# Output projection of the sliding-window layer as seven half-size products, with their operands summed during the attention

## The chip, the cores and the metric

The kernel runs on one core of a Trainium2 chip. A core has a matrix engine (TensorE, PE in the profile; PEld is its weight load), VectorE (DVE), ScalarE (ACT), GpSimd (POOL) and SyncE (SP), which here only issues DMA transfers. Each engine works through its own list of instructions in order and waits on semaphores for the others. Matmuls read from SBUF and accumulate in the eight banks of PSUM. The metric is the time of one execution in microseconds; lower is better.

## What is computed

Two layers over x of 1024 x 1024, fp32. Only the second is changed much:

```python
# even layer: RG-LRU heads and stick-breaking attention heads, gated, concatenated
y = concat([a_h * silu(a_g), o_b * silu(b_g)]);  x = LN(alpha * x + y @ w_out)      # w_out 2048 x 1024
# odd layer: 16 heads of 64, window 128, 2 key/value heads, sinks, ALiBi
q, k, v, g = split(x @ w_in)
p = softmax_with_sink(q @ k.T / 8 - slope * dist)                                      # inside the window
y = (p @ v) * silu(g);                               x = LN(alpha * x + y @ w_out)      # w_out 1024 x 1024
```

The kernel keeps fp32 precision by splitting each matmul operand into a high part h (rounded) and a low part l = raw - h, and adding three matmuls: h h, h l and l h (`mm3`, lines 110 to 112).

## The kernel before, in words

Data are in tiles of 128 partitions. A "slot" is one of 24 tiles of 128 x 2 x 512 that most operands share. The stages in order of time:

1. Projections of the even layer, its recurrent heads, and then eight heads of stick-breaking attention (`attn_all`). Each unit of a head is one score tile: three matmuls (L326 to 328), two sigmoids on ACT (L333), a running product on DVE (L342) and a product (L344); two units later the tile is transposed on PE (L352) and split (L118, L119). Between units a generator (`fill.pump`) feeds matmuls of other work to PE: the next head's projections, and in head 7 the first product of the output projection (`early_out`).
2. The even output projection (16 x 128 rows of w_out) is done as seven products of half size after Strassen and Winograd: `PRODUCTS` lists for each the y operand, the weight operand and one of two groups of four PSUM banks (X, Z). Sums of y pieces (`y_sums`) and of w_out pieces (`w_sums`, L268 to 283: four loads, five POOL operations, an ACT cast) are made during the attention, w_sums(n) late in head n, and stored to DRAM (`stash`). `prep(k)` loads the two operands of step k, casts the high parts on ACT (L541) and subtracts the low parts on DVE (y) and POOL (weights) (L543), nine steps ahead of `step_mm`. Normalisation of a row block: `bn_stats`, `bn_aggr`, square root, ACT scaling (L662), POOL multiplication by gamma (L663), DVE addition of beta (L668).
3. The odd layer: projections, then `swa_all`: eight pairs of heads with eight query blocks (units) each. A unit is four score matmuls (L900, L901), bias and maximum on DVE (L906), exponentials on ACT (L913), normalising on POOL (L918); three units later transposes on PE (L928) and the split pth / ptl (L118 on ACT, L119 on DVE), one unit later the attention matmuls (L946, L949). After two units the output is copied (L954), added (L957) and multiplied by its gate into the tile yo (POOL, L959). The fillers are the gate projection og of the same pair and the query projection oq of the next.
4. The odd output projection: the eight yo tiles are split (L1017 on ACT, L1018 on DVE), then 8 row blocks x 8 pieces of w_out x 2 column halves x 3 = 384 matmuls. Its first column half is mixed into pair 7 by the scheduler; the second goes row block by row block, each followed by its normalisation (L623 to L654), the last row block in two pieces of 256 columns.

The order of instructions on each engine is set when the kernel is built, by a scheduler that simulates the program; the loops only give the priorities.

Of the kernel before, what the change touches and what calls it, by code (L numbers as in the profile page):

```python
# [52 lines left out]
def trunk(ctx, tc, x, xT_in, w_even, w_even_v, w_even_out, w_gate, lru_vec,  # L53
# [560 lines left out]
    def out_proj(w_src, es, yh, n_tail, tail_piece, lnp, gb, after, name, final):  # L614
        def parts(s):
            return 4 if final and s == NS - 1 else 2

        stats = {s: lnp.tile([P, parts(s), 6], F32, tag=f"st{s}", name=f"st{name}{s}", bufs=1) for s in range(NS)}

        def evac(dm, s, ps, cols=(0, HALF)):  # L620
            c0, c1 = cols
            xt = xpre[:, s, dm * HALF + c0:dm * HALF + c1]
            nc.vector.scalar_tensor_tensor(out=xt, in0=xt, scalar=ALPHA, in1=ps[:, c0:c1], op0=ALU.mult, op1=ALU.add)  # L623
            w = D // parts(s)
            for c in range(0, c1 - c0, w):
                nc.vector.bn_stats(stats[s][:, (dm * HALF + c0 + c) // w, :], xt[:, c:c + w])

        def ln_a(s):
# [4 lines left out]
            return mv, rs  # L633

        def ln_b(s, mv, rs):
            nc.vector.reciprocal(rs[:, 0:1], rs[:, 0:1])
# [1 line left out]
            nmr = None
            if final and s == NS - 1:
                nmr = nc.vector.scalar_tensor_tensor(out=rs[:, 1:2], in0=mv[:, 0:1], scalar=-1.0, in1=rs[:, 0:1],  # L640
                                               op0=ALU.mult, op1=ALU.mult)
                a = slice(LNC, D)
                nc.scalar.activation(xt[:, a], xt[:, a], AF.Identity, bias=rs[:, 1:2], scale=rs[:, 0:1])
                nc.gpsimd.tensor_tensor(out=xt[:, a], in0=xt[:, a], in1=gb[:, 0, a], op=ALU.mult)
                nc.gpsimd.tensor_tensor(out=xt[:, a], in0=xt[:, a], in1=gb[:, 1, a], op=ALU.add)
            if final:
                edges = (0, LNC // 2, LNC) if s == NS - 1 else (0, 512, 1024)
                for c0, c1 in zip(edges, edges[1:]):
                    cs = slice(c0, c1)
                    m = nc.vector.scalar_tensor_tensor(out=xt[:, cs], in0=xt[:, cs], scalar=mv[:, 0:1],  # L650
                                                       in1=gb[:, 0, cs], op0=ALU.subtract, op1=ALU.mult)
                    if c0:
                        order(m, nmr)
                    nc.vector.scalar_tensor_tensor(out=xt[:, cs], in0=xt[:, cs], scalar=rs[:, 0:1], in1=gb[:, 1, cs],  # L654
                                                   op0=ALU.mult, op1=ALU.add)
                    after(s, cs)
                if s == NS - 1:
                    after(s, slice(LNC, D))
                return
            nc.vector.scalar_tensor_tensor(out=rs[:, 1:2], in0=mv[:, 0:1], scalar=-1.0, in1=rs[:, 0:1],  # L660
                                           op0=ALU.mult, op1=ALU.mult)
            nc.scalar.activation(xt, xt, AF.Identity, bias=rs[:, 1:2], scale=rs[:, 0:1])  # L662
            nc.gpsimd.tensor_tensor(out=xt, in0=xt, in1=gb[:, 0, :], op=ALU.mult)  # L663
# [418 lines left out]
```

## Time and profile before

| | us |
|---|---|
| median of 3 runs (lowest to highest) | 1248.36 (1248.14 to 1249.49) |
| profiled execution | 1249.23 |
| its span | 1247.5 |
| PE busy | 1223.2 (98%) |
| DVE, ACT, POOL busy | 849.5 (68%), 627.2 (50%), 623.5 (50%) |
| chain that ended last | PE 88%, DVE 6%, ACT 3% |

The mean granted clock of the execution is 0.998, so PE runs at 2.4 GHz nearly everywhere. The 16 DMA engines are half idle or more except where large operands move. Busy shares are means over stages; the stretches of 10 or 20 us below show where PE is idle.

### The profile page before, as it was taken

Reading aid. Unit: us, or ns where it says so; the run is one execution under the profiler, and the core shown is the slowest. Engines: PE = TensorE matmul, PEld = TensorE weight load, DVE = VectorE, ACT = ScalarE, POOL = GpSimd, SP = SyncE. Lnnn points to the kernel's source line nnn. Section 1 sums busy time; section 2 is a strip of 40 time slices with the busy share of each in tenths; the row PEclk is TensorE's granted clock in tenths of the full one; section 3 lists DMA queues with packets and bytes.
Section 4 is the critical chain, followed back from the end, with each engine's and each line's share of the span. In section 5 each row is a group of like instructions: output and inputs, shape, how many; then the busy total and the mean of one; then the engine's idle time right before and its main releaser. Section 6 shows DMA issues by size and latency. Waiting matters only on the chain.

```text
span 1247.5 us, 18450 instructions
## 1 busy us (share of the span) xinstructions
PE 1223.2 (98%) x6176; PEld 1035.3 (83%) x6176; DVE 849.5 (68%) x1705; ACT 627.2 (50%) x1291; POOL 623.5 (50%) x720
## 2 busy tenths in 40 slices
PE   8999999999999999999999899999999999999997
PEld 6888788888888888888888788888888888887886
DVE  8465666557776776767767728586468778778377
ACT  5255565556443443434444436444367777778300
POOL 3344354435536465554551647567346555555440
PEclk9999999999999999999999999999999999999999
DMA  7312433235515245254353988701111111111022
GB/s 258 123 56 80 148 106 106 91 108 183 172 51 186 92 168 180 74 181 154 109 178 132 383 328 300 249 26 43 43 44 35 34 35 34 28 34 61 21 81 102
DMA packets 88943, 150.16 MB, mean 120 GB/s; under 512 B 10128, under 2 KB 27920, under 8 KB 88592
## 3 DMA queue, kind: packets, MB, share of 16 engines
q1 hardware_dynamic: 88848, 148.98, 35.6%
q8 instruction: 49, 0.80, 0.3%
q14 instruction: 46, 0.38, 0.1%
HBM read 104.90 MB, written 44.04 MB: 119 GB/s over the span
## 4 chain that ended last, share of the span: by engine, by line
PE 88%; DVE 6%; ACT 3%; issue 1%; DMA 1%; POOL 0%; POOLq 0%; SPq 0%; ACTq 0%; DVEq 0%
PE pjv L110 2%; PE tr L352 2%; PE pjv L111 2%; PE pjv L112 2%; PE opeX L554 2%; PE pj_k L110 2%; PE pj_q L110 2%; PE pj_q L112 2%; PE opeX L555 2%; PE pj_k L112 2%; PE pj_k L111 2%; PE pj_q L111 2%; PE pj_g L111 2%; PE opeX L556 2%; PE pj_g L112 2%; PE pj_g L110 2%
## 5 line engine op out<-in xcount | busy, mean ns | idle before, releaser
L333 ACT ACTIVATE C<-z 128x512 f32<-128x512 f32 (+3 forms) x96 | 47.4, 494 | 107.6 <-DVE z L330 67.5
L918 POOL TENSOR_SCALAR S<-S,sm 128x256 f32<-128x256 f32 (+1 forms) x128 | 59.7, 481 | 70.1 <-DVE sm L916 23.9
L543 POOL TENSOR_TENSOR opwl<-rawwl,opwl 128x512 fp32r<-128x512 f32 x48 | 69.4, 1459 | 42.3 <-ACT opwl L541 25.3
L913 ACT ACTIVATE S<-S,sm 128x256 f32<-128x256 f32 (+1 forms) x128 | 62.5, 489 | 48.9 <-DVE sm L909 46.9
L344 DVE TENSOR_TENSOR B<-B,C 128x512 f32<-128x512 f32 (+3 forms) x96 | 75.0, 783 | 9.9 <-DVE wt L119 0.2
L342 DVE TENSOR_TENSOR_SCAN C<-C,one 128x512 f32<-128x512 f32 (+1 forms) x64 | 62.2, 973 | 21.2 <-ACT C L333 21.1
L342 DVE TENSOR_TENSOR_SCAN C<-C,C,one 128x512 f32<-128x512 f32 x32 | 44.1, 1378 | 30.0 <-ACT C L333 30.0
L543 DVE TENSOR_TENSOR opwh<-rawwh,opwh 128x512 fp32r<-128x512 f32 x48 | 51.5, 1101 | 16.0 <-ACT opwh L541 13.6
L118 ACT CAST wt<-tr 128x512 fp32r<-128x512 f32 (+3 forms) x96 | 46.4, 484 | 30.5 <-PE tr L352 30.0
L119 DVE TENSOR_TENSOR wt<-tr,wt 128x512 fp32r<-128x512 f32 (+3 forms) x96 | 52.3, 547 | 7.4 <-ACT wt L118 7.0
L110 PE MATMUL pjv<-wv,xh 128*128 128x512 f32 x128 | 49.6, 399 | 6.4 <-ACT wv L219 4.8
L381 POOL TENSOR_TENSOR yb<-pvt,yb 128x128 f32<-128x128 f32 x32 | 16.1, 503 | 76.2 <-DVE pvt L380 76.2
L541 ACT CAST opwh<-rawwh 128x512 fp32r<-128x512 f32 x48 | 29.8, 621 | 47.2 <-DMA rawwh<-stS 27.8
L110 PE MATMUL pj_g<-xh,wh_g 128*128 128x512 f32 x128 | 52.6, 411 | 0.0
L110 PE MATMUL pj_k<-xh,wh_k 128*128 128x512 f32 x128 | 51.9, 405 | 0.0
L110 PE MATMUL pj_q<-xh,wh_q 128*128 128x512 f32 x128 | 51.8, 405 | 0.0
L112 PE MATMUL pj_g<-xh,wl_g 128*128 128x512 f32 x128 | 51.8, 405 | 0.0
L110 PE MATMUL pj_oq<-x1h,wh_oq 128*128 128x512 f32 x128 | 51.6, 404 | 0.0
L110 PE MATMUL pj_og<-x1h,wh_og 128*128 128x512 f32 x128 | 51.5, 402 | 0.0
L111 PE MATMUL pj_og<-x1l,wh_og 128*128 128x512 f32 x128 | 50.8, 397 | 0.0
L112 PE MATMUL pj_og<-x1h,wl_og 128*128 128x512 f32 x128 | 50.7, 396 | 0.0
L111 PE MATMUL pjv<-wv,xh 128*128 128x512 f32 x128 | 50.7, 396 | 0.0
(333 smaller groups left out, 4386.6 us busy)
## 6 DMA issues: line engine op xcount, KB each, us to landing
vst<-vhl SPq DMA_DIRECT2D x16, 512.0 KB, 4.1
rawwh<-stS SPq DMA_DIRECT2D x32, 256.0 KB, 3.7
rawwl<-stT SPq DMA_DIRECT2D x32, 256.0 KB, 4.5
xraw<-in_xT_dram SPq DMA_DIRECT2D x16, 256.0 KB, 5.4
wvraw<-in_w_even_v_dram SPq DMA_DIRECT2D x16, 256.0 KB, 4.6
wr_ax<-in_w_even_dram SPq DMA_DIRECT2D x16, 256.0 KB, 2.7
wr_ag<-in_w_even_dram SPq DMA_DIRECT2D x16, 256.0 KB, 2.7
stA11p<-a SPq DMA_DIRECT2D x8, 512.0 KB, 2.8
```

The costliest lines, as they stand in the source:

```text
L110: nc.tensor.matmul(ps, wh, xh, start=start, stop=False)
L111: nc.tensor.matmul(ps, wh, xl, start=False, stop=False)
L112: nc.tensor.matmul(ps, wl, xh, start=False, stop=stop)
L118: nc.scalar.copy(h, ps)
L119: nc.vector.tensor_tensor(out=l, in0=ps, in1=h.bitcast(F32), op=ALU.subtract)
L333: nc.scalar.activation(C[:, :W], z[:, :W], AF.Sigmoid, scale=-SC)
L342: nc.vector.tensor_tensor_scan(cr, cr, one.broadcast_to([P, W]), init, ALU.mult, ALU.mult)
L344: nc.vector.tensor_tensor(out=B[:, :W], in0=B[:, :W], in1=C[:, 1:W + 1], op=ALU.mult)
L541: nc.scalar.copy(hl[:, 0, :], raw)
L543: eng.tensor_tensor(out=hl[:, 1, :], in0=raw, in1=hl[:, 0, :].bitcast(F32), op=ALU.subtract)
L913: nc.scalar.activation(Sb[:, j, lo:], Sb[:, j, lo:], AF.Exp, bias=nm[:, j:j + 1], accum_out=den[:, j:j + 1])
L918: nc.gpsimd.tensor_scalar(out=Sb[:, j, lo:], in0=Sb[:, j, lo:], scalar1=rec[:, j:j + 1], scalar2=0.0, op0=ALU.mult, op1=ALU.add)
```

## The change

The odd output projection (1024 x 1024 by 1024 x 1024) becomes seven products of half size: 7 products x 4 steps of depth 128 x 4 row blocks x 3 = 336 matmuls. k counts the steps, 0 to 27; product i = k // 4. The weight sums are made in pairs 0 to 3 (`w_sums(p, w_odd_out, 4, "o")` at unit 3: four loads, four POOL operations, four stores), the sums of y after units 3 and 7 of each pair (`y_sums_odd`: one POOL operation in pairs 0 to 3, three in pairs 4 to 7, and stores). `prep_odd` loads both operands of a step, casts on ACT and subtracts on DVE and POOL. Product 0 is started as a filler in pair 7 on three of four row blocks (`early_odd`); one half of pair 7's gate projection goes to pair 6 for it. The last two row stages run row block by row block with the normalisation of the even layer (`out_norms` serves both layers); only the last row block (row 3) has its normalisation shared among ACT, POOL and DVE as before, and its columns are no longer split for the matmuls. The even `w_sums(n + 1)` is made in head n, so head 0 makes two and head 7 none. Slots go from 24 to 27; a smaller DMA scratch area makes room.

```diff
-    slots = ctx.enter_context(tc.tile_pool(name="slots", bufs=24))
+    slots = ctx.enter_context(tc.tile_pool(name="slots", bufs=27))
...
+    def w_sums(t, src, half, o=""):
...
+        for tile_, dm, e in ((b22, 1, half + t), (b12, 1, t), (b11, 0, t), (b21, 0, half + t)):
+            nc.sync.dma_start(tile_, src[dm, e])
...
+        stash(o + "T3", t, b22)
+        if not o:
+            stash_parts("B11p", t, b11, slot(f"wb11{t}", F32R), nc.gpsimd)
...
-                if (i, g) == (NS - 2, 1):
-                    w_sums(n)
+                if (i, g) == (NS - 2, 1) and n < 7:
+                    w_sums(n + 1, w_even_out, 8)
+                if n == 0 and (i, g) == (2, 0):
+                    w_sums(0, w_even_out, 8)
...
+    def prep_odd(k, pool_=None):
+        i, t = divmod(k, 4)
+        yop, w_op, _ = PRODUCTS[i]
+        kinds = (("wh", yst["o" + yop.rstrip("p"), t]),
+                 ("wl", yst["o" + w_op, t] if w_op[0] == "T" else w_odd_out[ODD_W[i][0], ODD_W[i][1] + t]))
+        res = []
+        for tag, src in kinds:
+            raw = wpool.tile([P, HALF], F32, tag=tag, name=f"oraw{tag}{k}", bufs=5)
+            nc.sync.dma_start(raw, src)
+            hl = slot(f"oop{tag}{k}", F32R) if pool_ is None else \
+                pool_.tile([P, 2, HALF], F32R, tag="es", name=f"oop{tag}{k}", bufs=8)
+            nc.scalar.copy(hl[:, 0, :], raw)
+            eng = nc.vector if tag == "wh" else nc.gpsimd
+            eng.tensor_tensor(out=hl[:, 1, :], in0=raw, in1=hl[:, 0, :].bitcast(F32), op=ALU.subtract)
+            res.append(hl)
+        ops_o[k] = res
...
+    def step_odd(k, p):
+        i, t = divmod(k, 4)
+        y, w = ops_o[k]
+        c = slice(p * P, (p + 1) * P)
+        fresh = t == 0 and i in (0, 1, 5)
+        f = partial(nc.tensor.matmul, skip_group_check=True)
+        b = oop[PRODUCTS[i][2], p]
+        f(b, y[:, 0, c], w[:, 0, :], start=fresh, stop=False)
+        f(b, y[:, 0, c], w[:, 1, :], start=False, stop=False)
+        f(b, y[:, 1, c], w[:, 0, :], start=False, stop=t == 3)
...
+    ODD_W = {0: (0, 0), 5: (0, 4), 6: (1, 4)}
...
-    def out_proj(w_src, es, yh, n_tail, tail_piece, lnp, gb, after, name, final):
...
+    def out_norms(lnp, gb, after, name, final):
...
+        def evac(p, b, half, dm, first, done):
+            s = half * 4 + p
+            xt = xpre[:, s, dm * HALF:(dm + 1) * HALF]
+            if first:
+                nc.vector.scalar_tensor_tensor(out=xt, in0=xt, scalar=ALPHA, in1=b, op0=ALU.mult, op1=ALU.add)
+            else:
+                nc.vector.tensor_tensor(out=xt, in0=b, in1=xt, op=ALU.add)
+            if done:
+                nc.vector.bn_stats(stats[s][:, dm, :], xt)
...
+        def shift():
+            if pend:
+                s = pend.pop()
+                xt = xpre[:, s, :]
+                nc.vector.tensor_tensor(out=xt, in0=xt, in1=gb[:, 1, :], op=ALU.add)
+                after(s, slice(0, D))
...
+        def norm(s):
...
+            shift()
...
+            a = slice(LNC if final and s == LAST else 0, D)
+            nc.scalar.activation(xt[:, a], xt[:, a], AF.Identity, bias=rs[:, 1:2], scale=rs[:, 0:1])
+            nc.gpsimd.tensor_tensor(out=xt[:, a], in0=xt[:, a], in1=gb[:, 0, a], op=ALU.mult)
+            if not (final and s == LAST):
+                pend.append(s)
                 return
...
+            elif p == PAIRS - 1:
+                yield from proj_half(og[p], 1, f"og{p}", ev)
+                yield from early_odd()
...
+            if p + 2 == PAIRS:
+                og[p + 1] = w_ftile(w_odd, 11 + p, f"og{p + 1}")
+                yield from proj_half(og[p + 1], 0, f"og{p + 1}", evac_gate(("o", p + 1)))
...
+        def y_sums_odd(p, hf):
+            y, t = ytile["o", p], p % 4
+            tt = nc.gpsimd.tensor_tensor
+            if hf == 0:
+                stash(("oA11", "oA12")[p // 4], t, y[:, 0, :])
+                return
+            if p < 4:
+                if t % 2 == 0:
+                    s3o[t // 2] = slot(f"s3o{t}", F32)
+                s3 = s3o[t // 2][:, t % 2, :]
+                tt(out=s3, in0=y[:, 0, :], in1=y[:, 1, :], op=ALU.subtract)
+                stash("oS3", t, s3)
+                return
+            s3, y1 = s3o[t // 2][:, t % 2, :], ytile["o", t]
+            stash("oA22", t, y[:, 1, :])
+            tt(out=s3, in0=y[:, 1, :], in1=s3, op=ALU.subtract)
+            stash("oS2", t, s3)
+            tt(out=y1[:, 1, :], in0=y1[:, 1, :], in1=y[:, 1, :], op=ALU.add)
+            stash("oS1", t, y1[:, 1, :])
+            tt(out=y1[:, 0, :], in0=y[:, 0, :], in1=s3, op=ALU.subtract)
+            stash("oS4", t, y1[:, 0, :])
...
+        def early_odd():
+            for t in range(4):
+                prep_odd(t)
+            for p in range(3):
+                oop[0, p] = bank(XB[p], f"opoX{p}")
+            for t in range(4):
+                for p in range(3):
+                    step_odd(t, p)
+                    yield C_512
...
+                if n % 4 == 3:
+                    y_sums_odd(p, n // 4)
...
-                        orate[0] = (20.8 if p else 15.6) / 8 if p + 1 < PAIRS else 10.4 / 9
+                        orate[0] = {0: 15.6, PAIRS - 2: 26.0, PAIRS - 1: 13.4}.get(p, 20.8) / 8
...
+                    if p < 4 and n == 3:
+                        w_sums(p, w_odd_out, 4, "o")
...
-    for p in range(PAIRS):
-        raw = ytile["o", p]
-        h, l = slot(f"yho{p}", F32R), slot(f"ylo{p}", F32R)
-        nc.scalar.copy(fl(h), fl(raw))
-        nc.vector.tensor_tensor(out=fl(l), in0=fl(raw), in1=fl(h).bitcast(F32), op=ALU.subtract)
-        yhl["o", p] = (h, l)
...
-    out_proj(w_odd_out, list(range(8)), yh_odd, 8, lambda ti, src, nm: load_piece(src, nm, pool=slots),
-             ep, gb2, after_odd, "o", True)
...
+    oop[0, 3] = bank(XB[3], "opoX3")
+    for t in range(4):
+        step_odd(t, 3)
+    for k in range(4, 12):
+        prep_odd(k)
+    for p in range(4):
+        evac_odd(0, p)
+    for p in range(4):
+        oop[1, p] = bank(ZB[p], f"opoZ{p}")
+    for i in (1, 2):
+        for t in range(4):
+            prep_odd(4 * i + t + 8)
+            for p in range(4):
+                step_odd(4 * i + t, p)
+        for p in range(4):
+            evac_odd(i, p)
+    for rows, pair in ((4, (3, 4)), (0, (5, 6))):
+        for p in range(4):
+            if rows:
+                prep_odd(20 + p, ep)
+                prep_odd(24 + p)
+            else:
+                oop[1, p] = bank(ZB[p], f"opoY{p}")
+            for i in pair:
+                for t in range(4):
+                    step_odd(4 * i + t, p)
+                evac_odd(i, p)
+            norm(rows + p)
+    shift()
...
+    nc = _bacc.Bacc("TRN2", target_bir_lowering=False, num_devices=1, dynamic_dma_scratch_size=1024)
```

POOL at the end of the even attention, before: wq7a, wq7b and wb are the tiles of w_sums(7), C_j_0 the tiles of head 7's units (the memsets count them down to C_0_0, the last), yb the output tile of a head.

```order
L336 MEMSET C_4_1_6882 128x1
L275 TENSOR_TENSOR wq7b<-wq7b,wq7a 128x512
L336 MEMSET C_3_0_6937 128x1
L278 TENSOR_TENSOR wq7a<-wq7a 128x512
L264 TENSOR_TENSOR wb_6685<-wq7a,wb_6685 128x512
L336 MEMSET C_2_0_6962 128x1
L381 TENSOR_TENSOR yb_6584<-pvt_3_6871,yb_6584 128x128
L336 MEMSET C_1_0_7021 128x1
L280 TENSOR_TENSOR wq7a<-wq7b,wq7a 128x512
L282 TENSOR_TENSOR wq7b<-wq7b,wq7a 128x512
L336 MEMSET C_0_0_7047 128x1
```

After, the same operations, now among the units of head 6 and the weights (wh_g, wl_g) of head 7's gate projection:

```order
L102 TENSOR_SCALAR wh_g_0_6503<-wr_g_0_6501 128x512
L103 TENSOR_TENSOR wl_g_0_6504<-wr_g_0_6501,wh_g_0_6503 128x512
L337 MEMSET C_4_1_6355 128x1
L275 TENSOR_TENSOR wq7b<-wq7b,wq7a 128x512
L102 TENSOR_SCALAR wh_g_1_6509<-wr_g_1_6507 128x512
L279 TENSOR_TENSOR wq7a<-wq7a 128x512
L264 TENSOR_TENSOR wb_6151<-wq7a,wb_6151 128x512
L103 TENSOR_TENSOR wl_g_1_6510<-wr_g_1_6507,wh_g_1_6509 128x512
L281 TENSOR_TENSOR wq7a<-wq7b,wq7a 128x512
L382 TENSOR_TENSOR yb_6115<-pvt_3_6344,yb_6115 128x128
L283 TENSOR_TENSOR wq7b<-wq7b,wq7a 128x512
L337 MEMSET C_3_0_6443 128x1
```

The five operations on wq7 and wb have left the stretch before C_0_0 of head 7.

ACT in pair 7, after: oopwh and oopwl are the operands of a step k (the number behind the name), S7_2 the scores of pair 7's unit 2, pth6_6 the transposed weights of pair 6's unit 6, tmp6_5 the copies of an attention output.

```order
L574 CAST oopwh6_12252<-orawwh6_12250 128x512
L574 CAST oopwl6_12257<-orawwl6_12255 128x512
L928 ACTIVATE sm7_1_11802<-sm7_1_11802 128x2
L574 CAST oopwh7_12262<-orawwh7_12260 128x512
L574 CAST oopwl7_12267<-orawwl7_12265 128x512
L118 CAST pth6_6_11819<-ptr6_6_11814 128x512
L574 CAST oopwh8_12272<-orawwh8_12270 128x512
L971 COPY tmp6_5_11790<-opv6_4_11741 64x256
L972 COPY tmp6_5_11790<-opv6_4_11741 64x256
L930 ACTIVATE S7_2_11842,sm7_2_11843<-S7_2_11842,sm7_2_11843 128x256 x2
L928 ACTIVATE sm7_2_11843<-sm7_2_11843 128x2
```

Before, seven casts of the yo tiles stood in pair 7; now casts of step operands stand between the exponentials and the pth casts.

SP after the last attention output (yo7), after the change: st names are stores to DRAM, gb2 the gamma and beta of the last layer, orawwh the loads of y operands.

```order
L260 DMA stoA223_12192<-yo7_11699 128x512
L1034 DMA gb2_12207<-in_o_ln_dram 128x2048
L260 DMA stoS23_12195<-s3o2_10158 128x512
L260 DMA stoS13_12198<-yo3_10091 128x512
L260 DMA stoS43_12201<-yo3_10091 128x512
L571 DMA orawwh11_12300<-stoS23_12195 128x512
L571 DMA orawwh12_12318<-stoA220_11019 128x512
```

The load for k = 11 reads what the third of these rows stores, and stands behind the two stores after it; before, only gb2 was loaded here.

DVE at the end, before: sto are statistics of a row block, mv and rs its mean and factors, opo_7 and opo_7b the last row block's two pieces.

```order
L636 RECIPROCAL rs<-rs 128x1
L623 SCALAR_TENSOR_TENSOR xpre<-xpre,opo_7_12595 128x256
L654 SCALAR_TENSOR_TENSOR xpre<-xpre,rs,gb_11982 128x512 x2
L626 BN_STATS sto_12023<-xpre 128x6
L623 SCALAR_TENSOR_TENSOR xpre<-xpre,opo_7b 128x256
L626 BN_STATS sto_12023<-xpre 128x6
L631 BN_AGGR mv<-sto_12023 128x2
L650 SCALAR_TENSOR_TENSOR xpre<-xpre,mv,gb_11982 128x384
```

After: opoY and opoX are the last row block's two banks, the 128x1024 addition the beta of the row block before it.

```order
L661 TENSOR_TENSOR xpre<-opoY_12849,xpre 128x512
L669 TENSOR_TENSOR xpre<-xpre,gb_12207 128x1024
L663 BN_STATS sto_12212<-xpre 128x6
L659 SCALAR_TENSOR_TENSOR xpre<-xpre,opoX_12217 128x512
L663 BN_STATS sto_12212<-xpre 128x6
L669 TENSOR_TENSOR xpre<-xpre,gb_12207 128x1024
L675 BN_AGGR mv<-sto_12212 128x2
L691 SCALAR_TENSOR_TENSOR xpre<-xpre,mv,gb_12207 128x384
L678 RECIPROCAL rs<-rs 128x1
```

One addition of 1024 columns now stands between the last statistics and their BN_AGGR; the additions after the last matmul are on 512 columns.

## Rows read from the trace of the kernel before

**Rows 1.** Stretches: range, length, PE, PEld, DVE, ACT, POOL, clock, DMA share, GB/s.

```profile
690.00:700.00 10.00, 6.34 (x31) 5.30 (x30) 10.00 (x17) 4.80 (x14) 7.56 (x8) 0.83 1.00 368
820.00:840.00 20.00, 20.00 (x90) 16.57 (x89) 16.84 (x15) 7.80 (x11) 17.25 (x7) 1.00 0.00 1
960.00:980.00 20.00, 19.95 (x117) 17.32 (x117) 16.03 (x55) 16.98 (x41) 11.14 (x19) 1.00 0.12 29
1120.00:1140.00 20.00, 20.00 (x125) 17.61 (x123) 15.93 (x63) 15.80 (x44) 10.49 (x18) 1.00 0.10 26
1140.00:1160.00 20.00, 17.35 (x92) 13.94 (x91) 17.63 (x46) 18.17 (x42) 11.46 (x15) 1.00 0.22 79
```

**Rows 2.** Chain of waits, end of the odd projection: start us, us, what.

```profile
1224.88 0.23 PE opo L111
...
1233.94 0.23 PE opo L112
...
1239.96 0.43 DVE xpre L623
1240.41 0.44 DVE sto L626
```

**Rows 3.** DVE's time line in head 7's stall: start us, us, what.

```profile
691.01 1.18 DVE L344 TENSOR_TENSOR B<-B,C 128x512 f32<-128x512 f32 x1
...
692.70 1.70 DVE L342 TENSOR_TENSOR_SCAN C<-C,one 128x512 f32<-128x512 f32 x1
...
695.11 1.36 DVE L344 TENSOR_TENSOR B<-B,C 128x512 f32<-128x512 f32 x1
696.39 2.02 DVE L342 TENSOR_TENSOR_SCAN C<-C,one 128x384 f32<-128x384 f32 x1
```

**Rows 4.** DVE's groups by form, 520 to 680 us: busy us, mean ns.

```profile
L344 DVE TENSOR_TENSOR B<-B,C 128x512 f32<-128x512 f32 x19 | 17.7, 932 | 1.8
...
L342 DVE TENSOR_TENSOR_SCAN C<-C,one 128x512 f32<-128x512 f32 x6 | 7.7, 1290 | 2.9 <-ACT C L333 2.9
...
L342 DVE TENSOR_TENSOR_SCAN C<-C,one 128x384 f32<-128x384 f32 x7 | 6.7, 958 | 3.9 <-ACT C L333 3.8
```

**Rows 5.** Time line of POOL in the same stall.

```profile
689.57 2.06 POOL L278 TENSOR_TENSOR wq7a<-wq7a 128x512 f32<-128x512 f32 x1 [0.23 <-DMA wq7a<-in_w_even_out_dram]
```

**Rows 6.** Chain of waits behind the stall.

```profile
698.25 0.43 PE opeX L554
...
699.36 0.23 PE opeX L554
```

**Rows 7.** POOL's groups by form, 980 to 1080 us (odd attention).

```profile
L959 POOL TENSOR_TENSOR yo<-tmp,yo 128x256 f32<-128x256 f32 x12 | 8.8, 736 | 8.4 <-DVE tmp L957 8.4
L103 POOL TENSOR_TENSOR wl_og<-wr_og,wh_og 128x512 fp32r<-128x512 f32 x6 | 7.8, 1293 | 0.5
```

**Rows 8.** ACT's groups by form, 1080 to 1173 us (the pairs 6 and 7).

```profile
L1017 ACT CAST yho<-yo 128x1024 fp32r<-128x1024 f32 x7 | 7.3, 1038 | 0.0
...
L954 ACT COPY tmp<-opv 64x256 f32<-64x256 f32 x11 | 4.1, 370 | 5.1 <-PE opv L949 4.9
```

**Rows 9.** Page, costliest groups: the casts of the even projection.

```profile
L541 ACT CAST opwh<-rawwh 128x512 fp32r<-128x512 f32 x48 | 29.8, 621 | 47.2 <-DMA rawwh<-stS 27.8
```

**Rows 10.** DMA issues: KB each, median us from issue to landing.

```profile
rawwh<-stS SPq DMA_DIRECT2D x32, 256.0 KB, 3.7
...
stS<-yain SPq DMA_DIRECT2D x16, 256.0 KB, 2.0
```

**Rows 11.** Time line of POOL in the even projection.

```profile
758.03 14.32 POOL L543 TENSOR_TENSOR opwl<-rawwl,opwl 128x512 fp32r<-128x512 f32 x9 [0.21 <-ACT opwl L541]
```

**Rows 12.** Time line of DVE beside the even normalisation.

```profile
826.35 2.83 DVE L543 TENSOR_TENSOR opwh<-rawwh,opwh 128x512 fp32r<-128x512 f32 x1
...
831.41 0.68 DVE L543 TENSOR_TENSOR opwh<-rawwh,opwh 128x512 fp32r<-128x512 f32 x1
...
838.87 1.23 DVE L668 TENSOR_TENSOR xpre<-xpre,gb 128x1024 f32<-128x1024 f32 x1
```

More of the change, by code (lines that the diff above doesn't have):

```diff
@@ L612, in trunk @@
     LNC = 768
-    def out_proj(w_src, es, yh, n_tail, tail_piece, lnp, gb, after, name, final):
[L615 to L628, printed above, removed]
+    LAST = 3
+    def out_norms(lnp, gb, after, name, final):
+        stats = {s: lnp.tile([P, 2, 6], F32, tag=f"st{s}", name=f"st{name}{s}", bufs=1) for s in range(NS)}
+        pend = []
+        def evac(p, b, half, dm, first, done):
[14 more added lines that the diff above has]
+        def norm(s):
             mv = lnp.tile([P, 2], F32, tag="mv", name="mv", bufs=3)
@@ L632, in ln_a @@
             nc.scalar.activation(rs[:, 0:1], mv[:, 1:2], AF.Sqrt, bias=eps_t)
-            return mv, rs
-        def ln_b(s, mv, rs):
+            shift()
             nc.vector.reciprocal(rs[:, 0:1], rs[:, 0:1])
+            nmr = nc.vector.scalar_tensor_tensor(out=rs[:, 1:2], in0=mv[:, 0:1], scalar=-1.0, in1=rs[:, 0:1],
+                                                 op0=ALU.mult, op1=ALU.mult)
             xt = xpre[:, s, :]
[L638 to L658, printed above, removed]
-                return
[L660 to L663, printed above, removed]
@@ new lines, in norm @@
+            a = slice(LNC if final and s == LAST else 0, D)
[3 more added lines that the diff above has]
+                pend.append(s)
+                return
+            nc.gpsimd.tensor_tensor(out=xt[:, a], in0=xt[:, a], in1=gb[:, 1, a], op=ALU.add)
+            for c0, c1 in ((0, LNC // 2), (LNC // 2, LNC)):
+                cs = slice(c0, c1)
+                m = nc.vector.scalar_tensor_tensor(out=xt[:, cs], in0=xt[:, cs], scalar=mv[:, 0:1],
+                                                   in1=gb[:, 0, cs], op0=ALU.subtract, op1=ALU.mult)
+                if c0:
+                    order(m, nmr)
+                nc.vector.scalar_tensor_tensor(out=xt[:, cs], in0=xt[:, cs], scalar=rs[:, 0:1], in1=gb[:, 1, cs],
+                                               op0=ALU.mult, op1=ALU.add)
+                after(s, cs)
@@ L711, in trunk @@
+            after(s, a)
+        return evac, norm, shift
     ln_ctx = ExitStack()
@@ L735, in trunk, with even_products @@
     AHEAD = 9
[L737 to L738 removed]
+    def even_products():
+        put, norm, shift = out_norms(lnp, gb, lambda s, cs: None, "e", False)
         def evac(i, p):
[L741 to L759 removed]
+            put(p, op[PRODUCTS[i][2], p], *EVAC[i])
         op[0, 3] = bank(XB[3], "opeX3")
@@ L796, in even_products @@
                     x1_transposes(p + 1)
[L797 to L799 removed]
+            shift()
+    even_products()
     ln_ctx.close()
```

105 lines of the change are left out of this document (18 added, 87 removed).

## The prediction

> **What bounds the kernel now.** I read the page's busy shares first, then the busy time of each engine in short stretches, because an average over stages says little here. TensorE (PE) is busy 98% of the span, so only two things can shorten the run: fewer matmuls, or less PE idle time at the few places that have any. The stretches show where [rows 1]: PE is full at 820 to 840 and at 1120 to 1140, misses 0.05 us in 960 to 980, loses 3.66 us in 690 to 700 with a granted clock of 0.83, and 2.65 us in 1140 to 1160, where ACT is busy 18.17 of 20 us and DVE 17.63. The chain of waits gives the price of a matmul and the length of the end [rows 2]: 40 full matmuls of the odd output projection start between 1224.88 and 1233.94, so one takes 0.2265 us; the last is done when DVE's last addition starts at 1239.96, and the span ends at 1247.5.
>
> **The change part by part.** The sum is made against the profiled execution, 1249.23 us, of which 1247.5 is the span and 1.7 lies around it; the median of the three runs is 1248.36, so I subtract 0.87 at the end.
>
> *48 matmuls less.* The odd output projection goes from 8 x 8 x 2 x 3 = 384 matmuls to 7 x 4 x 4 x 3 = 336. All are on PE, which is full around them: 48 x 0.2265 = -10.9. The last row block was two half-width pieces before, with the same PE time.
>
> *Even weight sums one head ahead.* At the end of head 7 the five POOL operations of w_sums(7) run beside the last stages of the stick product on DVE. One of them starts at 689.57 and takes 2.06 us [rows 5], and DVE is full and slow in the same microseconds [rows 3]: against the mean of the same forms in the heads before [rows 4], the two multiplications are 1.18 + 1.36 - 2 x 0.93 = 0.7 longer, the scans 1.70 - 1.29 = 0.4 and 2.02 - 0.96 = 1.1: 2.2 us on the chain that PE waits for. After that wait PE ran at half clock for a moment: at 698.25 two matmuls in a row took 0.43 where the next take 0.23 [rows 6], 0.4 together. With the sums gone from head 7 (the order of POOL has them in head 6, where PE has projections to run): -2.6. The bounds are 0 (head 6 pays) and -5 (most of the idle goes). Head 0 has two sets of sums; at nothing, since its attention has a whole head's projections as cover; if that fails, it is five operations that DVE's scans meet, 2 us.
>
> *Sums in the odd attention, pairs 0 to 6.* Pairs 0 to 3 get four POOL operations for the weights and one for y, pairs 4 to 6 three for y. One costs 1.29 [rows 7]: 6.5 and 3.9 us a pair. POOL is busy 11.14 of 20 us there, DVE 16.03, PE 19.95 [rows 1], so POOL has room; the delay that counts is a softmax tile standing behind four such operations, 5.2 us, and the attention runs three units ahead of its transposes. I take +0.5, bounds 0 and +3; the price without that cover is the slower rival.
>
> *Pair 7.* Before, this pair carried the roundings of the y tiles: 7 ACT casts of 1.04 up to the last attention output [rows 8] and as many DVE subtractions. Now it carries 22 ACT casts of 0.62 [rows 9] for the operands of k = 0 to 10, with a DVE and a POOL subtraction for each pair of casts. On ACT that is 22 x 0.62 - 7 x 1.04 = 13.6 - 7.3 = +6.3 us. ACT was free for 4.2 + 1.83 = 6.0 us in 1120 to 1160 [rows 1], so it becomes full, and casts stand in its queue between the exponentials and the casts of the transposed weights (pth) that PE waits for. PE lost 2.65 us there before; I take +2.5, bounds 0 (the room holds it) and +6 (all of it late).
>
> *The wait at k = 11.* This is new. Product 2 needs S2 of pair 7, which is made from the last attention output. From the end of the last attention matmul: two copies of 0.37 (ACT), two DVE additions of the same half tiles, taken at as much, the gate product 0.74, and then three POOL operations of 1.29, all of which come before the load in SP's queue, since that load stands behind the stores of their three results (and behind the 1 MB of gb2): 0.74 + 0.74 + 0.74 + 3.87 = 6.1 [rows 7, 8]; the load itself 3.7 [rows 10], the cast 0.62: 10.4 us. If the store of the third result had to land first, it would be 2.0 more [rows 10]. PE has 33 matmuls before k = 11, 33 x 0.2265 = 7.5 us. So PE waits about 2.9, bounds 0 (the first of the 33 wait themselves for an evacuation, and the chain ends meanwhile) and +6 (with the landing and gb2's traffic in front). In PE's order the k = 11 matmuls stand ahead of all that follows, so nothing passes them; on ACT the casts of k = 12 and 13 are queued behind the cast of k = 11.
>
> *Operands k = 11 to 27.* Each pair of operands costs POOL and DVE a subtraction. In the even projection nine POOL ones ran in 14.32 us [rows 11], 1.6 each, where PE needs 12 x 0.2265 = 2.7 a pair: they keep ahead once running. Normalisation beside them was slow in the even layer (a DVE subtraction of 2.83, where the next took 0.68 [rows 12]), and yet PE was full at 820 to 840 [rows 1]. So +0.5, bounds 0 and +6.5 (rival C).
>
> *The end.* The last row block is no longer split: addition and statistics on 512 columns instead of 256 after the last matmul, 0.43 + 0.44 before [rows 2], half as much again on top: +0.5 (twice would be +0.9). And the shift of row 2 (128x1024) now stands ahead of the last bn_aggr on DVE, which the order shows. The same operation of the even layer takes 1.23 where POOL leaves it alone [rows 12]: +1.2. Together +1.7, bounds +0.5 (the shift done while the statistics wait for PE) and +3.8 (the shift held up as long as the 2.83 above).
>
> Sum: -10.9 - 2.6 + 0.5 + 2.5 + 2.9 + 0.5 + 1.7 = -5.4. Profiled execution 1243.8, median 1243.0.
>
> **The rivals.**
>
> B, *the waits are covered*: ACT's 6 us of room hold the casts, and the chain to k = 11 fits into the 7.5 us of matmuls in front of it. For it: PE ran the even projection, built in the same way, without a gap. Against: the even one had its operands nine steps ahead and no product that needs the last attention output. Without 2.5 + 2.9 + 0.5 + 0.5: 1243.0 - 6.4 = 1236.6.
>
> C, *DVE and POOL hold each other up in the row stage*: the 16 subtractions for rows 0 to 3 stand in front of and between the row blocks' additions and statistics. At 826.35 DVE lost 2.83 - 0.68 = 2.15 us on one subtraction [rows 12]; three such collisions on PE's path are 6.5: 1243.0 - 0.5 + 6.5 = 1249.0, no change. Against it: PE full at 820 to 840. The Trainium skill ("SBUF — State Buffer", section "Who interferes with whom") makes of this a rule without exception: a DVE instruction with two SBUF inputs and a GpSimd instruction that reads SBUF shut each other out for a whole instruction. The 2.83 agrees with it. By the rule a pair of operands takes 0.68 + 1.29 = 1.97 us and not 1.6, the 17 pairs 33.5, still within PE's 17 x 2.7 = 46; so the sum stays, but every addition behind such a pair is late, and for that C keeps a chance that the full PE at 820 to 840 alone would not leave it.
>
> D, *POOL sets the pace of the odd attention* (the slower one): each sum stands in POOL's queue ahead of a softmax tile that PE's transposes wait for. There are 4 x 6.5 + 3 x 3.9 = 37.7 us of new POOL work; if a third gets through to PE, +12.6 less the 0.5 counted: 1255.1. It decides from about a quarter on (9.4: 1251.9). For it: the transposes wait only for POOL's result, and ACT and DVE are close to full too. Against: three units of lead, and POOL is idle for 8.9 of 20 us.
>
> E, *the even sums only move their harm* to head 6, and the rest goes as forecast: 1243.0 + 2.6 = 1245.6, or 1247.6 with the 2 us for head 0.
>
> **How the numbers follow.** Forecast 0.48, with its own range 1238.5 to 1246.5; B 0.20; C 0.14; D 0.13; E 0.05. A measurement of this kernel can tell about 0.2% from no change, so faster is below 1245.9 and slower above 1250.9. Faster: 0.44 of the forecast, 0.20 of B, 0.01 of C: 0.65. No change: 0.04 + 0.11 + 0.05 (E) = 0.20. Slower: 0.02 of C and 0.13 of D: 0.15. The range of eight in ten takes in B and C: 1235.5 to 1250.5.
>
> **What would show it.** Right: 48 matmuls fewer; at the end of head 7 DVE's scans back at 1.3 and 0.96 and PE's idle there halved; pairs 0 to 6 at the old pace with POOL near 15 of 20 us; ACT at 20 of 20 in pair 7; one PE wait of 2 to 5 us for the cast of k = 11; 9 us from the last matmul to the end. Wrong: transposes that wait for POOL in every pair (D), PE waiting for operand subtractions between row blocks (C), or a wait at k = 11 long enough that the granted clock falls after it, as at 690 to 700: then each matmul run at the low level costs 0.2 us more, and the loss is more than the wait.

## The result, and the profile after

The changed kernel takes 1263.01 us (median of four runs, 1262.05 to 1263.98) where the kernel before, on the same chip, takes 1248.92 (four runs, one more than in the table above). The ratio is 1.0111 [1.0094, 1.0129]: 14 us slower. The forecast was 1243.0, with a range up to 1250.5, and 0.15 for slower.

The stretches of the profile after come first (range, length, busy time of PE, PEld, DVE, ACT and POOL with instruction counts, granted clock, DMA share, GB/s), to be laid beside [rows 1]:

```profile
690.00:700.00 10.00, 9.30 (x59) 8.14 (x58) 9.39 (x21) 5.13 (x14) 1.73 (x4) 1.00 1.03 416
...
960.00:980.00 20.00, 18.72 (x105) 15.44 (x103) 15.88 (x46) 15.57 (x38) 16.68 (x23) 1.00 0.48 159
...
1140.00:1160.00 20.00, 16.24 (x83) 13.50 (x84) 18.20 (x53) 14.81 (x43) 15.18 (x20) 0.91 0.41 116
1180.00:1200.00 20.00, 12.39 (x42) 9.33 (x41) 8.60 (x8) 6.96 (x13) 10.93 (x9) 0.74 0.79 239
1220.00:1240.00 20.00, 20.00 (x90) 16.56 (x89) 18.95 (x35) 6.57 (x10) 11.81 (x5) 1.00 0.20 79
1240.00:1261.60 21.60, 2.23 (x10) 1.50 (x8) 16.93 (x29) 4.87 (x7) 9.37 (x5) 0.65 0.31 121
```

The reader is to see four things. At 690 to 700 PE has won 2.96 us (9.30 where it had 6.34). At 1180 to 1200, the start of the odd output projection, it has lost about half of the stretch: 42 matmuls where it can run some 90. From 1220 to 1240 it is full, and looks as good as before. And from 1240 on there are 21.6 us with almost no matmul in them, in which DVE is the busiest.

The time line gives the two ends of the projection's trouble (start us, us, what; the bracket is the idle time before and what ended it):

```profile
1192.97 2.07 PE L587 MATMUL opoX<-oopwl,oopwh 128*128 128x512 f32 x4 [6.83 <-ACT oopwl L574]
1196.55 0.63 PE L588 MATMUL opoX<-oopwl,oopwh 128*128 128x512 f32 x1
1196.97 0.63 PE L589 MATMUL opoX<-oopwl,oopwh 128*128 128x512 f32 x1
...
1241.84 0.39 PE L589 MATMUL opoX<-oopwl,oopwh 128*128 128x512 f32 x1
```

PE waits 6.83 us for the operand of k = 11, and then matmuls follow each other at 0.42 us instead of 0.2265 [rows 2]. The last one ends at 1242.2, 2.3 us later than before (1239.9), and the span then goes on for another 19.4 us where it was 7.6.

### The profile page after: what moved, and what is told of

It is laid out like the page before. It is cut to its first block, busy times and chain, and to the rows that moved or that the text cites. A ratio compares the mean times of both kernels' runs of the same rounds, so it can differ in the third digit from the quotient of the medians.

```text
span 1261.6 us, 18662 instructions
## 1 busy us (share of the span) xinstructions
PE 1217.3 (96%) x6104; PEld 1026.8 (81%) x6104; DVE 891.8 (71%) x1720; ACT 660.0 (52%) x1346; POOL 699.6 (55%) x755
## 4 chain that ended last, share of the span: by engine, by line
PE 84%; DVE 8%; ACT 4%; DMA 2%; issue 2%; POOL 1%; POOLq 0%; SPq 0%; ACTq 0%; DVEq 0%
PE pjv L110 2%; PE pjv L111 2%; PE tr L353 2%; PE pjv L112 2%; PE pj_k L110 2%; PE pj_q L110 2%; PE pj_k L112 2%; PE pj_q L112 2%; PE pj_k L111 2%; PE pj_q L111 2%; PE pj_g L111 2%; PE pj_g L112 2%; PE pj_g L110 2%; PE opeX L557 2%; PE opeX L558 2%; PE opeX L559 2%
## 5 line engine op out<-in xcount | busy, mean ns | idle before, releaser
L546 POOL TENSOR_TENSOR opwl<-rawwl,opwl 128x512 fp32r<-128x512 f32 x48 | 75.3, 1592 | 27.4 <-ACT opwl L544 27.3
L546 DVE TENSOR_TENSOR opwh<-rawwh,opwh 128x512 fp32r<-128x512 f32 x48 | 65.3, 1396 | 22.0 <-ACT opwh L544 21.9
L343 DVE TENSOR_TENSOR_SCAN C<-C,one 128x512 f32<-128x512 f32 (+1 forms) x64 | 58.9, 920 | 21.6 <-ACT C L334 21.5
L684 POOL TENSOR_TENSOR xpre<-xpre,gb 128x1024 f32<-128x1024 f32 (+1 forms) x16 | 40.6, 2548 | 27.5 <-ACT xpre L683 27.3
L923 DVE CUSTOM_DVE_ANT_0 S<-s,bias 128x256 f32<-128x256 f32 (+1 forms) x128 | 47.0, 401 | 8.1 <-PE s L918 6.2
L112 PE MATMUL pjv<-wv,xl 128*128 128x512 f32 x128 | 50.8, 397 | 0.0
```

The lines of the kernel that those rows point to most:

```text
L112: nc.tensor.matmul(ps, wl, xh, start=False, stop=stop)
L343: nc.vector.tensor_tensor_scan(cr, cr, one.broadcast_to([P, W]), init, ALU.mult, ALU.mult)
L546: eng.tensor_tensor(out=hl[:, 1, :], in0=raw, in1=hl[:, 0, :].bitcast(F32), op=ALU.subtract)
L923: nc.vector.tensor_tensor_reduce(out=Sb[:, j, lo:], in0=ps[:, j, lo:], in1=bias[:, j, lo:], scale=1.0, scalar=-BIG, op0=ALU.add, op1=ALU.m ...
```

## The experiments

Each ratio is against the kernel before, run on the same chip; "last matmul" and "behind it" are from the profiled execution.

| kernel | median us | ratio [95%] | last matmul ends | behind it |
|---|---|---|---|---|
| before | 1248.92 | | 1239.9 | 7.6 |
| changed | 1263.01 | 1.0111 [1.0094, 1.0129] | 1242.2 | 19.4 |
| e1_even_ahead | 1242.29 | 0.9946 [0.9933, 0.9960] | 1232.4 | 7.5 |
| e2_even_own | 1268.76 | 1.0151 [1.0136, 1.0166] | 1248.8 | 19.2 |
| e3_no_s2 | 1253.13 | 1.0029 [1.0019, 1.0040] | 1232.8 | 18.4 |
| e4_gb2_late | 1256.59 | 1.0057 [1.0043, 1.0070] | 1236.9 | 19.1 |
| e6_no_late_sub | 1259.62 | 1.0080 [1.0066, 1.0093] | 1241.7 | 16.4 |
| e7_no_odd_wsums | 1260.70 | 1.0086 [1.0071, 1.0101] | 1240.5 | 19.2 |
| e8_pool_subs_norm_dve | 1271.74 | 1.0183 [1.0166, 1.0200] | 1241.7 | 27.8 |
| e9_norm_dve | 1263.61 | 1.0121 [1.0106, 1.0136] | 1240.9 | 20.4 |
| e10_no_shift | 1253.88 | 1.0037 [1.0025, 1.0049] | 1241.4 | 8.9 |
| e11_shift_behind | 1261.71 | 1.0102 [1.0087, 1.0117] | 1241.9 | 18.7 |
| e12_gb2_late_half_shift | 1258.51 | 1.0070 [1.0053, 1.0087] | 1233.7 | 21.8 |
| e16_three_out | 1241.48 | 0.9930 [0.9914, 0.9947] | 1230.3 | 11.1 |

Where a text below gives microseconds for a ratio, they are the difference of two ratios times 1249; with two intervals of some 0.0015 each, one such difference is good to about 3 us.

**e1: the even weight sums alone.** The kernel before, with only this edit in it:

```diff
-                if (i, g) == (NS - 2, 1): w_sums(n)
+                if (i, g) == (NS - 2, 1) and n < 7: w_sums(n + 1)
+                if n == 0 and (i, g) == (2, 0): w_sums(0)
```

> The kernel before, with only the even weight sums made one head ahead (two sets in head 0, none in head 7). If that part alone gives what the trace of the changed kernel shows (4.0 us less PE idle time between 680 and 720), it is 3.5 to 4.5 us faster than before: about 1244.5. If the harm only moves to heads 0 or 6, no change: 1247 to 1249.

It is 6.7 us faster, more than either forecast. In head 7's stretch PE is full, and DVE's operations run with no POOL operation longer than 0.1 us beside them (stretch; then DVE's time line):

```profile
690.00:700.00 10.00, 10.00 (x62) 8.73 (x61) 8.55 (x20) 4.96 (x13) 2.32 (x5) 1.00 1.03 414
```

```profile
692.61 0.68 DVE L344 TENSOR_TENSOR B<-B,C 128x512 f32<-128x512 f32 x1
693.21 0.95 DVE L342 TENSOR_TENSOR_SCAN C<-C,one 128x384 f32<-128x384 f32 x1
```

Before, these two took 1.18 to 1.36 and 2.02 [rows 3]. Of the means that the prediction set beside them [rows 4], the 0.93 of the multiplication held delays of its own; the 0.96 of the scan did not. Where the prediction had 2.6 us, PE's idle time falls by 3.7 in this stretch and by 1.6 in the rest of 680 to 720, and its busy time by 2.2 over the whole run (1223.2 to 1221.0). This is the best kernel of the study that computes the whole of the reference.

**e2: the odd half alone** (the even sums back in their own head).

```diff
-                if (i, g) == (NS - 2, 1) and n < 7: w_sums(n + 1, ...)
-                if n == 0 and (i, g) == (2, 0): w_sums(0, ...)
+                if (i, g) == (NS - 2, 1): w_sums(n, ...)
```

> The changed kernel with the even weight sums back in their own heads: the odd half alone. If the two halves add up (the even half alone gave 7.2 us), it is 7 us slower than the whole change: 1269 to 1271. If the odd half also frees head 7 in some way, or the even gain is partly lost in the whole change, 1264 to 1268.

The odd half by itself costs 1.51%, 18.9 us. This splits the result: some -5 (from here) to -7 (e1) for the even half, and +19 for the odd one.

**e3 and e4: the wait at k = 11.** In e3 the operand k = 11 is loaded from pair 6's stored tile instead of pair 7's, so its value is another; in e4 the 1 MB load of gb2 is issued later, and nothing is left out.

```diff
 e3:  yst[..., 2 if k == 11 else t]          # was: t
 e4: -    nc.sync.dma_start(gb2, ...)        # before the projection
     +            if (i, t) == (2, 0): order(nc.sync.dma_start(gb2, ...), odma["wh", 15])
```

> The changed kernel, but step k = 11 loads the sum of pair 6 in place of that of pair 7, so no step of product 2 waits for the last attention output (one operand is left out of the result). Theory 1 (the load for k = 11 blocks SP's queue until its store has landed, all later operands come late, and DVE works off their subtractions ahead of the row additions): the 6.8 us wait and the half-clock matmuls after it go (8 to 11 us), and the 19 us behind the last matmul shrink to 10 to 14: 1243 to 1250. Theory 2 (the end is long because of the new normalisation, ACT to POOL to DVE, whenever it starts): the wait goes, the 19 us stay: 1252 to 1255.

> The changed kernel, with the 1 MB load of gamma and beta issued behind the load for k = 15 instead of ahead of the store that k = 11 waits for. Theory 1, with the 1 MB as the reason why that store took 6.6 us: it lands in 2.5 to 3.5, the wait of PE falls from 6.8 to 2.5 to 4 us, and the total by 4 to 8: 1255 to 1259. If the 1 MB does not matter: 1262 to 1264.

Without the wait 10.2 us come back, more than the 6.8 of the wait itself. e3's stretch of the same 20 us holds 91 matmuls where the changed kernel's has 42:

```profile
1180.00:1200.00 20.00, 20.00 (x91) 16.55 (x90) 12.59 (x16) 9.76 (x19) 16.17 (x12) 1.00 0.77 274
```

49 matmuls of 0.2265 are 11.1 us: the wait, and the low clock behind it (0.74 on the mean of that stretch, 1.00 in e3; the 13 matmuls from 1192.97 to 1198.68 take 5.7 us instead of 2.9). The time behind the last matmul stays (18.4), so it is another matter. The chain of waits after (start us, us, what) says what the wait is made of:

```profile
1181.68 0.55 SPq L1034
...
1182.28 6.60 DMA stoS<-s3o
...
1188.93 2.75 DMA orawwh<-stoS
...
1191.78 0.58 ACT oopwh L574
```

The load must wait for the store to land, and the store takes 6.6 us. The DMA issues of 1176 to 1203 (count, KB each, median us to landing) show its neighbour in the queue; the second fence is e4's:

```profile
gb<-in_o_ln_dram SPq DMA_DIRECT2D x1, 1024.0 KB, 7.6
...
stoS<-s3o SPq DMA_DIRECT2D x1, 256.0 KB, 6.6
```

```profile
stoS<-s3o SPq DMA_DIRECT2D x1, 256.0 KB, 2.5
```

With gb2 out of the way the same store lands in 2.5 us, PE waits 2.1 instead of 6.8, and the kernel gains 6.7 us. So about two thirds of the cost of k = 11 comes from the 1 MB load in front of the store.

**e10, e11, e9, e12: the end, by the beta additions.** DVE adds beta (L669, 128x1024) in the normalisation that runs between the row blocks. e10 leaves these additions out for all row blocks but the last (row 3); e11 has each queued behind the row's factors instead of ahead of them; e9 has DVE do POOL's and ACT's share of the normalisation; e12 is e4 with four of the seven additions on POOL.

```diff
 e10: -  nc.vector.tensor_tensor(out=xt, in0=xt, in1=gb[:, 1, :], op=ALU.add)
      +  if not final: ...the same
 e11: +  if final: shift(nmr)                # behind the factors, not before the reciprocal
 e9:  +  if final and s != LAST: two DVE scalar_tensor_tensor per 512 columns; return
 e12: +  if final and s % 2 == 0: nc.gpsimd.tensor_tensor(out=xt, in0=xt, in1=gb[:, 1, :], op=ALU.add)
```

> The changed kernel without the addition of beta in the last normalisation, except for the last row block (seven DVE additions of 1024 columns are left out; in the changed kernel they took 11.6 us). Theory 1 (the 19 us behind the last matmul are DVE's work, which begins late): 8 to 12 us less, 1251 to 1255. Theory 2 (a row's statistics stand behind the addition for the row before, and that waits for ACT and POOL): the chain is broken, 4 to 8 us less, 1255 to 1259.

> The changed kernel with the same work, but in the last normalisation the addition of beta for the row block before stands behind the statistics and factors of a row and not ahead of them. Theory 1 (amount of DVE work): no change, 1261 to 1264. Theory 2 (order: the statistics wait for POOL through DVE's queue): 4 to 8 us less, 1255 to 1259.

> The changed kernel with the last normalisation as in the kernel before (four DVE operations of 512 columns a row block, none on ACT and POOL). DVE gets some 18 us of work in place of 11.6. Theory 1: 3 to 7 us slower, 1265 to 1270. Theory 2: no chain over three engines, 4 to 8 us faster, 1255 to 1259.

> The changed kernel with the load of gamma and beta behind the load for k = 15 (alone it gave 6.4 us), and the addition of beta for every second row block on POOL and not on DVE. If the end is set by the amount of DVE's work, four additions less (6 to 7 of the 11.6 us) shorten it by 3 to 5 us more: 1251 to 1254. If POOL then becomes the last, as it has 2.4 us more for each: 1256 to 1259.

e10 gives 9.2 us, and the time behind the last matmul falls to 8.9, while the last matmul itself moves by less than a microsecond: the end was DVE's work, not PE's. e11 (-1.1) cannot be told from nothing; its DVE order differs from the changed kernel's only from 1243 on, so it says that the order of the last row blocks doesn't matter. e9 (+1.2) cannot be told from nothing either, and missed both of its forecasts. DVE's time for the normalisation rises there from 11.6 us to 20.0 (groups by form, 1192 to 1261):

```profile
L684 DVE SCALAR_TENSOR_TENSOR xpre<-xpre,mv,gb 128x512 f32<-128x512 f32 x14 | 10.2, 770 | 0.0
L686 DVE SCALAR_TENSOR_TENSOR xpre<-xpre,rs,gb 128x512 f32<-128x512 f32 x14 | 9.8, 740 | 0.0
```

These 8.4 us more cost nothing, as far as the run can tell. So the amount of DVE's work alone isn't the cause: what it loses beside POOL and ACT counts too, and no run separates the two. e12 gains nothing over e4: POOL, which had waited between the row blocks, now runs almost without a gap to the end, with additions of 2.4 to 3.4 us beside DVE:

```profile
1227.26 3.40 POOL L686 TENSOR_TENSOR xpre<-xpre,gb 128x1024 f32<-128x1024 f32 x1
...
1251.42 0.72 POOL L692 TENSOR_TENSOR xpre<-xpre,gb 128x256 f32<-128x256 f32 x1
```

**e6 and e8: the subtractions among it.** In e6 the low part of the y operands k = 20 to 27 is a second ACT cast instead of a DVE subtraction (another value); in e8 the subtractions of k = 12 to 27 go to POOL and the normalisation to DVE, as in e9.

```diff
 e6: + if k >= 20 and tag == "wh": nc.scalar.copy(hl[:, 1, :], raw)   # no subtraction
 e8: - eng = nc.vector if tag == "wh" else nc.gpsimd
     + eng = nc.vector if tag == "wh" and k < 12 else nc.gpsimd
```

> The changed kernel without the DVE subtractions of the steps k = 20 to 27 (eight of them; the low parts of these y operands are a second ACT cast instead, so the low part is left out). Theory 1 (DVE is behind because these stand ahead of and between the row additions): the end behind the last matmul shrinks by 5 to 12 us: 1251 to 1258. Theory 2 (the chain of the normalisation sets it): under 3 us: 1260 to 1263.

> As the run with the last normalisation on DVE, and POOL alone does both operand subtractions from k = 12 on (2.6 us a step against PE's 2.7). DVE loses 16 subtractions that took 1.2 to 1.5 us each beside POOL. Theory 1: the end behind the last matmul falls to 8 to 11 us: 1251 to 1255, or a little more where PE waits for POOL. Theory 2: as the run without this, within 2 us.

Both missed. e6 gave 3.9 us and not 5 to 12: DVE now waited for square roots that stood behind the added casts in ACT's queue (waits of DVE: us, times, longest).

```profile
DVE rs L682 <- ACT rs L680: 6.9, 4, 4.9
```

e8 lost 9.0. Its DVE time line and POOL's, one fence each:

```profile
1220.62 1.27 DVE L661 TENSOR_TENSOR xpre<-opoX,xpre 128x512 f32<-128x512 f32 x2
...
1223.77 11.09 DVE L684 SCALAR_TENSOR_TENSOR xpre<-xpre,mv,gb 128x512 f32<-128x512 f32 x2
...
1234.96 1.35 DVE L684 SCALAR_TENSOR_TENSOR xpre<-xpre,mv,gb 128x512 f32<-128x512 f32 x2
```

```profile
1223.64 1.28 POOL L576 TENSOR_TENSOR oopwh<-orawwh,oopwh 128x512 fp32r<-128x512 f32 x1
1224.89 1.28 POOL L576 TENSOR_TENSOR oopwl<-orawwl,oopwl 128x512 fp32r<-128x512 f32 x1
...
1232.37 1.28 POOL L576 TENSOR_TENSOR oopwl<-orawwl,oopwl 128x512 fp32r<-128x512 f32 x1
```

Two DVE operations that read two SBUF operands took 11.09 us while POOL ran its subtractions without a gap; the next two took 1.35 once POOL had stopped. Additions that read PSUM (L661) took 0.64 each just before, with POOL's row of subtractions already running beside them. In this run, then, a DVE operation was held up for much longer than one POOL instruction. As a remedy for the end, e8 is a failure, and it also changed the order of the row blocks, so its 9 us aren't due to this one pair alone.

**e7: the sums in the odd attention.** The operands of the sum products are read from a slice of the stored weights instead of the sums, and pairs 0 to 3 make no weight sums (other values).

```diff
-                    if p < 4 and n == 3: w_sums(p, w_odd_out, 4, "o")
-  ("wl", yst["o" + w_op, t] if w_op[0] == "T" else ...)
+  ("wl", w_odd_out[0, t]    if w_op[0] == "T" else ...)
```

> The changed kernel without the weight sums in pairs 0 to 3 (their loads, POOL operations and stores are left out, and the plain weights are loaded in their place). If POOL's sums pace the pairs, the 2.0 us of PE waits between 940 and 1120 go and more with them: 1259 to 1261. If they are hidden, under 1 us: 1262 to 1264.

3.1 us, at the edge of what one difference can tell; PE's listed waits in 930 to 1125 fall from 2.0 to 0.8.

**e16: e3, e7 and e10 together.**

> The changed kernel with three of its costs left out at once: step k = 11 loads the sum of pair 6 (alone 9.9 us), no addition of beta in the last normalisation except for the last row block (alone 9.1), and no weight sums in pairs 0 to 3 (alone 2.3). If these are separate costs, they add up: 1263.0 - 21.3 = 1241 to 1243. If the wait at k = 11 and DVE's late work are one and the same, less than the sum: 1245 to 1250. Measured against the kernel with the even half alone (1242.3), what is left of the 10.9 us for 48 matmuls can then be read.

22.6 us, where the three alone sum to 10.2 + 3.1 + 9.2 = 22.5: they are separate costs and add. And yet e16 (0.9930) can't be told from e1 (0.9946), though it has 48 matmuls less. Its last matmul ends at 1230.3, 2.1 us before e1's. PE is busy for 1213.0 us (e1: 1221.0), so 8.0 of the 10.9 show in its busy time; the missing 2.9 fit matmuls at the low clock, and 5.9 are new idle time. Half of the idle time (2.9) lies in pair 7, from 1120 to 1180, where the clock falls too:

```profile
1140.00:1160.00 20.00, 16.51 (x81) 13.57 (x80) 17.43 (x49) 13.55 (x42) 14.27 (x17) 0.83 0.31 93
```

The rest is spread over head 7 (1.1), pairs 0 to 6 (0.8) and the projection (1.0). What of pair 7 the early casts cause, and what the weaker cover at its end, wasn't tried on its own and stays open.

## Why the prediction was wrong

The sign was wrong. Two terms of the sum failed, the wait at k = 11 and the end: 10.2 and 11.9 us where it had 2.9 and 1.7. These 17.5 us are most of the 19.5 between -5.4 and +14; the other terms were off by less, in both directions.

*"So PE waits about 2.9, bounds 0 ... and +6 (with the landing and gb2's traffic in front)."* Mis-sized: the wait is 6.83, above the upper bound, and its cost 9.9 to 10.2 us by e3. The chain was right, but the sum put the landing of the store at nothing, with 2.0 only as an "if" [rows 10]. The load waited for that landing, and it took 6.6 us, because the store stood behind 1 MB (e4: 2.5 without it). The low clock after the wait, which the last paragraph of the prediction named as what would make it wrong, added about 2.8.

*The end, "together +1.7"*, measured +11.9 (19.4 against 7.5 in e1). *"They keep ahead once running"* holds for what PE needs: behind k = 11 it waits for no operand that the list of its waits shows. The step that failed is the next one, *"and yet PE was full at 820 to 840"* [rows 1]: a full PE was taken to show that the whole row stage keeps up, so that DVE would begin the end with only one late shift. PE was full from 1220 to 1240 too, since it needs only the operands and free PSUM, and DVE fell behind all the same. In the even layer DVE was late as well, but it caught up before the last matmul. Its time line there:

```profile
836.47 1.27 DVE L748 TENSOR_TENSOR xpre<-opeZ,xpre 128x512 f32<-128x512 f32 x2
...
859.77 0.69 DVE L746 SCALAR_TENSOR_TENSOR xpre<-xpre,opeX 128x512 f32<-128x512 f32 x1 [1.27 <-PE opeX L556]
```

PE ended the last of the four products behind the first line at about 834.2, so DVE is behind there; the last addition of the layer, at 859.77, waits for PE. The stretches show the difference, before at the end of the even projection and after in the odd one (columns as above):

```profile
840.00:860.00 20.00, 20.00 (x107) 16.96 (x106) 15.71 (x31) 8.39 (x14) 9.08 (x7) 1.00 0.00 1
```

```profile
1200.00:1220.00 20.00, 20.00 (x90) 16.54 (x89) 19.93 (x21) 13.42 (x22) 19.42 (x13) 1.00 0.76 249
```

With eight steps in a product, the last two products of a row block are 48 matmuls (10.9 us at 0.2265); with four steps in the odd layer they are 24 (5.4 us), while DVE's additions, statistics and shift for a row block are the same. This is a count; no run tested it on its own. The costliest DVE groups of 1192 to 1262 by form (busy us, mean ns, idle before):

```profile
L576 DVE TENSOR_TENSOR oopwh<-orawwh,oopwh 128x512 fp32r<-128x512 f32 x17 | 22.8, 1369 | 9.0 <-ACT oopwh L574 9.0
L669 DVE TENSOR_TENSOR xpre<-xpre,gb 128x1024 f32<-128x1024 f32 x7 | 11.6, 1655 | 0.7 <-POOL xpre L684 0.7
L663 DVE BATCH_NORM_STATS2 sto<-xpre 128x6 f32<-128x512 f32 x16 | 11.0, 686 | 0.2
```

17 subtractions take 1.37 us each, twice the shortest in [rows 12], 0.68: the late operand k = 11 has held up the loads of k = 12 to 27 behind it in SP's queue, so their casts and subtractions come bunched, while POOL does the other half of them. (In e3, where they aren't held up, the mean is still 1.21.) DVE's time line shows what waits for them:

```profile
1210.08 0.68 DVE L661 TENSOR_TENSOR xpre<-opoZ,xpre 128x512 f32<-128x512 f32 x1
...
1217.10 0.68 DVE L661 TENSOR_TENSOR xpre<-opoX,xpre 128x512 f32<-128x512 f32 x1
...
1227.63 3.41 DVE L669 TENSOR_TENSOR xpre<-xpre,gb 128x1024 f32<-128x1024 f32 x1
...
1252.27 0.66 DVE L659 SCALAR_TENSOR_TENSOR xpre<-xpre,opoX 128x512 f32<-128x512 f32 x1
```

The addition at 1217.10 is for the first row block's second product, whose last matmul PE ended at about 1208.9 by its time line: 8 us late. The last addition starts at 1252.27, 10 us after the last matmul. The chain of waits shows how the rest of the span is spent:

```profile
1250.05 1.25 ACT xpre L683
...
1251.37 2.59 POOL xpre L684
...
1253.98 1.22 DVE xpre L669
1255.20 0.13 DVE mv L675
```

The long DVE operations in these lines are the collisions of rival C, which the prediction priced at three, 6.5 us on PE's path in the row stage, and gave 0.14; but the waits of PE that C expected between row blocks did not come. The Trainium skill ("SBUF — State Buffer", section "Who interferes with whom") was cited there for it; the trace agrees, with 1.37 for an SBUF subtraction against 0.68 for an addition from PSUM. What C lacked is that late DVE work, whether it is long by itself or by collisions, has no cover after the last matmul. e10 (-9.2) gives the price of the 7 additions: more than the 3.1 that they are longer than 7 of 1.22, so it isn't their collisions alone. e3 shows that without the late k = 11 the end stays at 18.4, so the bunching isn't needed for it.

*Even weight sums, -2.6:* the right sign, -6.7 by e1 (5.0 within the change, by e2). The delay was counted at 690 to 700 only, and one of the means that it was counted against was inflated itself.

*48 matmuls, -10.9:* they are gone from PE's order, but PE's busy time against e1 fell by 3.7 only; the other 7.2 fit the matmuls at the low clock (0.74 and 0.91 in the stretches above). Of these, 2.9 go with the wait at k = 11 (e3: PE busy for 1214.4 us instead of 1217.3); the rest no run took apart.

*Pairs 0 to 6, +0.5:* some 2 to 3 us (PE's idle time in 900 to 1120 rises from 0.05 to 2.2; e7's 3.1 agrees); PE loses 1.28 of 20 us at 960 to 980, with POOL at 16.68 (forecast: near 15). Rival D, with 12.6, did not happen. *Pair 7, +2.5:* about right. From 1120 to 1180 PE is idle for 5.9 us (1.23 + 3.76 + 0.94), before for 3.4; the clock of 0.91 in 1140 to 1160 comes on top. The waits of 900 to 1262 name the causes, of which the last two and 1.8 of the 3.0 are its own:

```profile
PE opoX L587 <- ACT oopwl L574: 6.8, 1, 6.8
PE opv L963 <- DVE tmp L974: 3.0, 2, 1.8
PE ptr L945 <- POOL S L935: 1.5, 1, 1.5
PE s L917 <- DVE sm L923: 1.2, 1, 1.2
```

No run isolates it. "ACT at 20 of 20" was not seen (18.23 in 1120 to 1140, then 14.81): in pair 7 these waits of PE are for DVE and POOL, not for ACT.

The sum against the profile, from e1's span to the changed kernel's: PE idle +13.5, PE busy -3.7, behind the last matmul +11.9, together +21.7 (1239.9 to 1261.6).

## What to carry to other kernels

A full PE in a row stage doesn't show that the vector engine keeps up; count its backlog at the last matmul, because with nothing behind it the vector work that is late there is added to the span. Matmuls that a change takes away were cover for that work: here PE's time for a row block's last two products is 5.4 us, where the layer that served as the model has 10.9. Before a new store-and-reload stands on the critical path, look at what is in front of it in the same DMA queue, and price the clock behind the wait as well as the wait. And change one half at a time: here the small half, which the forecast valued at 2.6 us, is the gain (6.7), and the large half the loss.

## What the runs showed that was not expected

Two DVE operations with two SBUF operands took 11.09 us (one of them 10.42) beside an unbroken row of POOL subtractions of 1.28 each (e8), where two take 1.35 without it. DVE's normalisation of 20.0 us costs no more than its share of 11.6 beside ACT and POOL (e9). A 256 KB store behind a 1 MB load landed in 6.6 us and without it in 2.5 (e4). Taking away a wait of 6.8 us gave back 10.2 (e3), as the granted clock fell behind it.
